# Retention heads of a one-core hybrid block: values and gates requested first, turned outputs stored from SyncE's queue and split half by half, index products one step later, selection steps spread over nearly every step

## The chip, the core and the metric

The kernel runs on one core of one Trainium2 chip. The metric is the device time of one execution in microseconds (us); a smaller number is better. The core's engines each work through their own instructions in order and wait for one another by semaphores: TensorE (PE in the profile, with its weight loads as PEld), VectorE (DVE), ScalarE (ACT), GpSimd (POOL) and SyncE (SP), which only issues DMA transfers here. GpSimd issues transfers too, and computes a little.

## The reference

One block of a language model in float32, for 512 tokens and 16 leading meta tokens, width 1024: a gated feed-forward, a mixer, a second gated feed-forward, and a norm. The mixer adds two branches:

```python
yr = retention(rope(rq), rope(rk) * RET_DK**-0.5, rv)      # 4 heads, keys of 256, values of 512
yr = (jax.nn.silu(rg) * yr) @ w_ret_out                     # yr is normalised per head first
ya = dsa_attention(rope(aq), rope(ak), av, rope(iq), rope(ik), iw, k_top) @ w_att_out
merged = jax.nn.sigmoid(g_ret) * yr + jax.nn.sigmoid(g_att) * ya
h = h + merged @ w_mix_out
```

Retention is attention without a softmax, with a decay in the distance of query and key. The sparse attention first scores all keys by eight small index heads (`relu(iq @ ik) * iw`, summed) and lets each query see its 128 best.

## The kernel before

**Numbers in two parts.** Every float32 operand of a matmul is split into a high part, rounded by ACT (`whi`, line 322), and the rest, by DVE (`wlo`, line 323). A product takes three matmuls: high by high, high by low, low by high. So a weight tile of 128x1024 needs a DMA, an ACT and a DVE instruction before TensorE may use it.

**Steps.** The program from the values' projections to the end of retention is one list of steps (`steps_through`, line 327). A step is one weight tile (128 columns and 8 row blocks, or 256 columns and 4 row blocks): its matmuls, and work of other engines "beside" it. In step i the weights of step i+4 are requested (one request serves two tiles; two buffers called `raw`), those of step i+2 are split, and the lower split is emitted inside the step, by `lower()`. PE, ACT, DVE and, in the part that matters here, SP keep exactly the order in which the code emits (`manual_schedule`); POOL's order is left to the scheduler.

**The stretch of the change** is from about 624 us to 945 us of the profile. Its steps in order: two gate tiles (`psgate`, the gates of the merge); queries and keys of head 1 (`psrq` twice, `psrk` twice); two more gate tiles; then, for each head h, four output steps (`psro`, line 155, called from line 1701) that multiply head h's outputs by `w_ret_out` and add them into eight accumulators `accr`; between the output steps of heads 0, 1, 2 and 3 stand the queries and keys of heads 2 and 3, and before head 3's outputs one tile each of the attention's keys and queries (`psak`, `psaq`) and two gates. While head h is multiplied out, head h+1 is prepared: its gates pass SiLU (`open_gates`), its values are split (`values_in`, line 1487), its keys are roped (`rope_pieces`), its scores decayed (`decayed`, `psst`), and its weighted values computed (`weigh`, `pspv`).

**A head's way out.** `weigh` computes, for four blocks of 128 queries, an output tile in PSUM, its sum of squares (ACT, line 1567) and its product with the gate (DVE, line 1569). After each pair of blocks GpSimd makes the norm's factor (`osum`, line 1574), ACT scales (`normed`), and DVE transposes within 32x32 blocks into `cross` (`turn`, line 1588); four transfers carry `cross` to DRAM (`ots`, lines 1591 and 1592), and one reads it back so that it lies with values on the partitions (`fetch_turned`, `land`, line 1596). `arrived` (line 1752) splits `land` into the two parts of `o`, which the output steps read. A head has two halves of this, `leave_half(h, 0)` from within `weigh_all` and `leave_half(h, 1)` in `trip` (line 1743). The first output matmul reads all 512 tokens of `o`, that is both halves.

**What a head needs first.** `fetch_head` (line 1471) requests a head's values (`vrs`) and gates (`rgs`), 2 MB; `new_decay` its decay table; `place_tails` (line 1367) the meta tokens' values, by GpSimd. For head 0 these stand in `bring_more` and `bring_index`, which the first two gate steps call, with the index heads' queries (`ia`, `ib`: 768 KB each), rope tables and the causal mask.

**Index work.** `index_steps` (line 1298) is a generator: each `pair()` runs one piece, first a small transpose, then ten pieces of four (or eight) matmuls `pssc`, whose results ACT passes through ReLU and DVE adds into `score`. `select_steps` (line 1327) is another: each of its 48 steps, run by `pick(n)`, is a MAX8 and a MATCH_REPLACE8 on DVE that find a row's next eight best scores, sixteen over 512 keys, sixteen over 384, sixteen over 256. What is left of it when the steps end is emitted after them and woven into the attention's start.

PSUM has four banks called `sm` (`pool("mxsm", 4, PSUM)`), which `psgate`, `psrq`, `pssc`, `psst`, `pspv` and `psro` share; a bank is free when ACT or DVE has read it.

## Time and profile before

| | us |
|---|---|
| median of 3 runs | 1543.68 (1543.65 to 1543.93) |
| the profiled execution, its own time | 1542.61 |
| its span, first to last instruction | 1540.8 |
| mean granted clock of TensorE, share of full | 0.984 |
| DVE busy over the span | 1140.2 |
| POOL busy over the span | 213.9 |

The profile of one execution gives for each engine its busy time, for groups of equal instructions their count, total and mean, and for each idle gap what released the engine (written `[idle us <-releaser]`). In the timeline's rows the columns are start, length (both us), engine, line of the kernel, operation, output and input, shape, and the gap before it. Names like `whi<-raw` are the tiles written and read. A row of the view by windows gives the stretch, its length, each engine's busy time with its count, then the granted clock of TensorE (1.00 is full speed), the DMA engines' busy share and GB/s. Lengths of matmul rows overlap, because matmuls are pipelined.

### The profile page before, as it was taken

The page shows a single profiled execution, that of the slowest core. Times are in us where ns is not written, and L with a number is a line of the kernel's source. Part 1 is how long each engine was busy: PE and PEld are TensorE (multiplying, and loading weights), DVE is VectorE, ACT ScalarE, POOL GpSimd, SP SyncE. Part 2 cuts the span into 40 slices and gives each one's busy share as a digit, 9 for nine tenths or more (in the row PEclk, how much of TensorE's full clock was granted, in tenths as well). Part 3 has the DMA queues.
Part 4 walks back from the last instruction along what each step waited for, and adds up shares of the span by engine and source line. Part 5 has one row for each costly group of instructions (what it writes and reads, how often), then busy time and mean ns, then how long its engine had stood idle before and what let it go on. Part 6 is the DMA issues. An engine that isn't in the chain of part 4 may idle for free.

```text
span 1540.8 us, 22309 instructions
## 1 busy us (share of the span) xinstructions
PE 1492.2 (97%) x8704; PEld 1306.3 (85%) x8704; DVE 1140.2 (74%) x1715; ACT 751.3 (49%) x1054; POOL 213.9 (14%) x320
## 2 busy tenths in 40 slices
PE   9999999999999999888989998999999999999997
PEld 8999999999888778776877777988888888888886
DVE  5987585776977877476787868878656787777676
ACT  5555353554454444445433435777634654444343
POOL 1000000002100001220202101344202311111110
PEclk9999999999999999989999999999999999999999
DMA  5233333237554441734335153577568476376423
GB/s 166 74 119 93 100 103 115 85 99 232 184 200 144 154 155 73 256 107 143 86 142 195 52 167 112 141 190 196 170 186 280 133 222 208 109 220 185 140 82 109
DMA packets 169914, 228.42 MB, mean 148 GB/s; under 512 B 18385, under 2 KB 115177, under 8 KB 169553
## 3 DMA queue, kind: packets, MB, share of 16 engines
q1 hardware_dynamic: 147872, 169.77, 34.3%
q0 software_dynamic: 17824, 49.86, 11.3%
q10 hardware_dynamic: 4112, 7.36, 1.4%
q8 instruction: 68, 1.11, 0.3%
q14 instruction: 38, 0.30, 0.1%
HBM read 187.17 MB, written 39.60 MB: 147 GB/s over the span
## 4 chain that ended last, share of the span: by engine, by line
PE 82%; DVE 9%; DMA 4%; ACT 2%; issue 2%; POOL 1%; SPq 0%; POOLq 0%; DVEq 0%; ACTq 0%
PE psqX L2279 7%; PE psd L2444 7%; PE psvX L1196 7%; PE psd L155 7%; PE psqX L155 6%; PE psvY L1196 4%; PE psro L155 4%; PE psqY L2279 4%; PE psqY L155 3%; PE psga L155 3%; PE psat L155 3%; PE psmo L155 3%; PE psak L155 3%; PE psaq L155 2%; DMA raw<-in_w_ret_out_dram 2%
## 5 line engine op out<-in xcount | busy, mean ns | idle before, releaser
L322 ACT ACTIVATE whi<-raw 128x1024 fp32r<-128x1024 f32 (+2 forms) x142 | 133.5, 941 | 137.9 <-PE psd L155 30.9
L323 DVE TENSOR_TENSOR wlo<-raw,whi 128x1024 fp32r<-128x1024 f32 (+2 forms) x142 | 156.1, 1102 | 51.3 <-ACT whi L322 51.3
L323 DVE TENSOR_TENSOR wlo<-w,whi 128x1024 fp32r<-128x1024 f32 x96 | 117.1, 1220 | 64.9 <-ACT whi L322 64.6
L322 ACT ACTIVATE whi<-w 128x1024 fp32r<-128x1024 f32 x96 | 101.6, 1058 | 110.2 <-PE psd L2444 39.3
L155 PE MATMUL psro<-o,whi 128*128 128x512 f32 x256 | 85.4, 414 | 16.7 <-DVE o L323 11.0
L155 PEld LDWEIGHTS psro<-o,whi 128*128 128x128 f32 x256 | 51.5, 201 | 30.3 <-DVE o L323 12.6
L155 PE MATMUL psd<-hl,whi 128*128 128x264 f32 x352 | 71.4, 284 | 0.0
L155 PE MATMUL psd<-hh,wlo 128*128 128x264 f32 x352 | 70.9, 283 | 0.0
L155 PE MATMUL psd<-hh,whi 128*128 128x264 f32 x352 | 70.8, 283 | 0.0
L115 ACT ACTIVATE whi<-raw 128x1024 fp32r<-128x1024 f32 (+1 forms) x42 | 43.5, 1036 | 46.8 <-PE psga L155 11.3
L155 PE MATMUL psqX<-th,whi 128*128 128x264 f32 x216 | 61.2, 283 | 0.2 <-DVE g L543 0.2
L155 PE MATMUL psqX<-tl,whi 128*128 128x264 f32 x216 | 61.2, 283 | 0.0
L155 PE MATMUL psqX<-th,wlo 128*128 128x264 f32 x216 | 61.2, 283 | 0.0
L2444 PE MATMUL psd<-whi,hl 128*128 128x512 f32 (+1 forms) x148 | 56.9, 384 | 0.1
L2444 PE MATMUL psd<-wlo,hh 128*128 128x512 f32 (+1 forms) x148 | 56.8, 384 | 0.0
L2444 PE MATMUL psd<-whi,hh 128*128 128x512 f32 (+1 forms) x148 | 56.8, 384 | 0.0
L116 DVE TENSOR_TENSOR wlo<-raw,whi 128x1024 fp32r<-128x1024 f32 (+1 forms) x42 | 49.9, 1189 | 8.7 <-ACT whi L115 8.6
L287 POOL TENSOR_TENSOR RR<-RR,sq 128x528 f32<-128x528 f32 x7 | 9.4, 1345 | 324.4 <-ACT sq L286 324.4
L155 PEld LDWEIGHTS psd<-hh,wlo 128*128 128x128 f32 x352 | 54.5, 188 | 0.0
L155 PEld LDWEIGHTS psd<-hh,whi 128*128 128x128 f32 x352 | 54.1, 188 | 0.0
L155 PEld LDWEIGHTS psd<-hl,whi 128*128 128x128 f32 x352 | 54.0, 188 | 0.0
L322 ACT ACTIVATE whi<-wsum 128x1024 fp32r<-128x1024 f32 x36 | 38.1, 1060 | 30.2 <-PE psd L155 14.7
(567 smaller groups left out, 4774.0 us busy)
## 6 DMA issues: line engine op xcount, KB each, us to landing
w<-in_w_in_dram SPq DMA_DIRECT2D x40, 512.0 KB, 5.3
raw<-in_w_in_dram SPq DMA_DIRECT2D x27, 512.0 KB, 4.1
raw<-in_w_in_dram SPq DMA_DIRECT2D x13, 1024.0 KB, 6.0
raw<-in_ffn_w_down_dram SPq DMA_DIRECT2D x24, 512.0 KB, 3.9
raw<-in_ffn_w_up_dram SPq DMA_DIRECT2D x11, 1024.0 KB, 5.2
raw<-in_ffn_w_gate_dram SPq DMA_DIRECT2D x10, 1024.0 KB, 5.1
ws<-in_ffn_w_up_dram POOLq DMA_DIRECT2D x20, 512.0 KB, 5.9
w<-in_ffn_w_up_dram SPq DMA_DIRECT2D x20, 512.0 KB, 5.7
```

What stands on the lines that cost most here:

```text
L115: nc.scalar.activation(hi, src, AF.Copy)
L116: eng.tensor_tensor(lo, src, hi.bitcast(F32), ALU.subtract)
L155: nc.tensor.matmul(o, a[:, k, :], b[:, sl], start=first and k == 0 and i == 0, stop=last and k == nk - 1 and i == 2, skip_group_check=onto)
L287: eng.tensor_tensor(ssum[:, :n], ssum[:, :n], sq[:, :n], ALU.add)
L322: nc.scalar.activation(hi, src, AF.Copy)
L323: return lambda: nc.vector.tensor_tensor(lo, src, hi.bitcast(F32), ALU.subtract)
L1196: nc.tensor.matmul(d[bank_][t], a, b[:, k, :], start=not onto and j + k + m == 0, stop=j + k == 3 and m == 2, skip_group_check=onto)
L2279: nc.tensor.matmul(ps[:, t], a, b[:, k, :], start=not onto and j + k + m == 0, stop=j + k == 3 and m == 2, skip_group_check=onto)
L2444: nc.tensor.matmul(ps, a, m[:, j, cs], start=first and i == 0, stop=last and i == 2)
```

## The change

Five edits, all of order or of the issuing queue; no arithmetic changes, and the number of instructions on PE, DVE and ACT stays as it was.

1. Head 0's decay table, values, gates, tails and the index keys are requested in the first gate step; the index queries, the rope tables and the mask in the second.
2. The four stores of a turned half go out on SP's queue instead of GpSimd's, and both read-backs are requested together in `trip`, after the second half's stores.
3. The values, gates and decay table of heads 2 and 3 are requested in the first output step of the head before, as head 1's were, not in `trip`; head 1's decay table moves there too.
4. `arrived` runs half by half: the first half a step earlier, the second where both stood; for head 0 both halves a step earlier (behind the third gate tile).
5. The index pieces start one step later (only the small transpose stays in the last key step) and are spread five to a gate step; selection steps stand in 26 of the 28 steps from head 0's outputs to head 3's, where they stood in 18, and 42 of the 48 come before head 3's outputs, where it was 29.

```diff
         def bring_index():
-            new_decay(0)
             nc.sync.dma_start(ia[:, :, :NL], fq[:, :, :NL])
...
                 nc.sync.dma_start(t, rope[0, i, :, REAL])
+            nc.sync.dma_start(caus, causal)
+            for i, t in enumerate((cos, sin)):
+                nc.sync.dma_start(t, rope[2, i])
 
         def bring_more():
+            new_decay(0)
             fetch_head(0)
+            place_tails(0)
             nc.gpsimd.dma_start(ka[:64, :S], fs[:64, 0, :])
...
             nc.gpsimd.dma_start(iw, fs[64 : 64 + IH, 0, :])
-            place_tails(0)
-            nc.sync.dma_start(caus, causal)
-            for i, t in enumerate((cos, sin)):
-                nc.sync.dma_start(t, rope[2, i])
@@ turn
-                nc.gpsimd.dma_start(d.rearrange("(b i) a e -> a i b e", i=32)[a],
+                nc.sync.dma_start(d.rearrange("(b i) a e -> a i b e", i=32)[a],
@@ outputs, step i
-                        fetch_head(1)
-                    if h == RH - 1 and i == 0:
+                    if i == 0 and h + 1 < RH:
+                        fetch_head(h + 1)
+                        new_decay(h + 1)
+                    elif i == 0:
                         vr["raw"] = fetch_values(4, vraw())
@@
         def leave_half(h, half):
             normed(h, half)
             turn(h, half)
-            fetch_turned(h, half)
@@ beside_outputs
                     some(heads[h + 1]["ropes"]["k"], (4, 3)[i])
-                else:
-                    pick(2)
+                pick((1, h == 0, 1 + (h == 0), 2 + (h == 0))[i])
@@
         def trip(h):
             leave_half(h, 1)
+            for half in range(2):
+                fetch_turned(h, half)
             if h + 1 < RH:
-                if h:
-                    fetch_head(h + 1)
                 place_tails(h + 1)
-                new_decay(h + 1)
 
-        def arrived(h):
-            for low in [turned_parts(h, half) for half in range(2)]:
+        def arrived(h, halves=(0, 1)):
+            for low in [turned_parts(h, half) for half in halves]:
                 low()
@@ the steps
         def start_0(w, lower):
-            bring_index()
+            bring_more()
...
         def start_1(w, lower):
-            bring_more()
+            bring_index()
...
-            arrived(0)
+
+        def after_2(ps):
+            later_gate(2)(ps)
+            arrived(0)
...
-        more += queries_keys(1, (beside_q0, beside_q1, beside_k0, nothing), ((), (), (), ((4, pair), (7, pair))))
-        more += steps_of(gr[2:4], [proj("psgate", REAL, ((1, pair), (3, pair), (5, pair), (7, pair)), later_gate(2)),
-                                   proj("psgate", REAL, ((1, pair), (3, pair), (5, pair), (7, pair)), after_3)])
+        more += queries_keys(1, (beside_q0, beside_q1, beside_k0, nothing), ((), (), (), ((7, pair),)))
+        five = tuple((i, pair) for i in (1, 2, 4, 5, 7))
+        more += steps_of(gr[2:4], [proj("psgate", REAL, five, after_2), proj("psgate", REAL, five, after_3)])
...
-            more += queries_keys(h + 1, (lambda h=h: trip(h), lambda: pick(2), lambda: pick(3), lambda h=h: (arrived(h), pick(1))))
+            more += queries_keys(h + 1, (lambda h=h: (trip(h), pick(2)), lambda: pick(1), lambda h=h: (arrived(h, (0,)), pick(2)),
+                                           lambda h=h: (arrived(h, (1,)), pick(2))))
...
-        more += steps_of(tiles("ak", w_in, OFF_AK, 1), [proj("psak", None, (), lambda ps: (first_kq.append(ps), trip(p)))])
-        more += steps_of(tiles("aq", w_in, OFF_AQ, 1), [proj("psaq", REAL, (), lambda ps: (first_kq.append(ps), pick(2)))])
-        more += steps_of(gr[4:6], [proj("psgate", REAL, (), lambda ps: (later_gate(4)(ps), pick(3))),
-                                   proj("psgate", REAL, (), lambda ps: (later_gate(5)(ps), arrived(p)))])
-        more += outputs(p, lambda i: pick(2 + (i == 0)))
+        more += steps_of(tiles("ak", w_in, OFF_AK, 1), [proj("psak", None, (), lambda ps: (first_kq.append(ps), trip(p), pick(2)))])
+        more += steps_of(tiles("aq", w_in, OFF_AQ, 1), [proj("psaq", REAL, (), lambda ps: (first_kq.append(ps), pick(3)))])
+        more += steps_of(gr[4:6], [proj("psgate", REAL, (), lambda ps: (later_gate(4)(ps), arrived(p, (0,)), pick(4))),
+                                   proj("psgate", REAL, (), lambda ps: (later_gate(5)(ps), arrived(p, (1,)), pick(4)))])
+        more += outputs(p, lambda i: pick(3))
```

How the order on the engines moves is shown at three places. The first is SP's queue in the first two gate steps (`u` is the decay table, `vl` and `g` head 0's values and gates, `ixs` the index queries). Before:

```order
L131 DMA raw<-in_w_in_dram 128x8x256
L1466 DMA u<-in_decay_dram 128x528
L1414 DMA ixs<-fq 128x4x384
L1419 DMA cos<-in_rope_dram 128x512
L1419 DMA sin<-in_rope_dram 128x512
L1479 DMA vl<-vrs 128x1024 x2
L1482 DMA g<-rgs 128x1024 x2
```

and now:

```order
L131 DMA raw<-in_w_in_dram 128x8x256
L1466 DMA u<-in_decay_dram 128x528
L1479 DMA vl<-vrs 128x1024 x2
L1482 DMA g<-rgs 128x1024 x2
L1413 DMA ixs<-fq 128x4x384
L1418 DMA cos<-in_rope_dram 128x512
L1418 DMA sin<-in_rope_dram 128x512
```

The values and gates have moved past the index queries and the index rope tables.

The second place is SP's queue from head 0's last output steps to the first output step of head 1 (`ots<-cross` are the stores, `land<-ots` the read-backs, `in_w_ret_out_dram` the output weights of head 1, `vraw` and `g` the values and gates of head 2). Before:

```order
L1596 DMA land<-ots 128x4x256
L131 DMA raw<-in_w_ret_out_dram 128x4x512
L1596 DMA land<-ots 128x4x256
L1479 DMA vraw<-vrs 128x1024 x2
L1482 DMA g<-rgs 128x1024 x2
L1466 DMA u<-in_decay_dram 128x528
L131 DMA raw<-in_w_ret_out_dram 128x4x512
```

and now:

```order
L1591 DMA ots<-cross 32x16x64 x4
L131 DMA raw<-in_w_ret_out_dram 128x4x512
L1591 DMA ots<-cross 32x16x64 x4
L1596 DMA land<-ots 128x4x256 x2
L131 DMA raw<-in_w_ret_out_dram 128x4x512
L131 DMA raw<-in_w_in_dram 128x8x256
L1479 DMA vraw<-vrs 128x1024 x2
```

The second request of output weights has moved ahead of head 2's values, gates and table, the first ahead of the first read-back; the eight stores are new in this queue.

The third place is ACT's queue around the end of the third gate tile (`RR<-psgate` is the gate's sigmoid, `tmp<-pssc` the ReLU of the index products, `o<-land` the high split of head 0's outputs). Before:

```order
L1319 ACTIVATE tmp<-pssc 128x384 x2
L1656 ACT_TABLE_LOAD
L1656 ACTIVATE RR<-psgate 128x512
L322 ACTIVATE whi<-raw 128x1024
L1319 ACTIVATE tmp<-pssc 128x384 x6
L1319 ACTIVATE tmp<-pssc 128x512 x2
L1656 ACTIVATE RR<-psgate 128x512
```

and now:

```order
L1319 ACTIVATE tmp<-pssc 128x384 x2
L1656 ACT_TABLE_LOAD
L1656 ACTIVATE RR<-psgate 128x512
L322 ACTIVATE o<-land 128x4x256 x2
L322 ACTIVATE whi<-raw 128x1024
L1319 ACTIVATE tmp<-pssc 128x384 x6
L1319 ACTIVATE tmp<-pssc 128x512 x4
```

The two splits of head 0's outputs now stand ahead of the last ten ReLUs, where they stood behind the last.

## The prediction

> **What bounds the kernel now.** I read the page's busy shares first, then TensorE's idle gaps in the stretch that the change touches, then the granted clock behind them, then who was late.
>
> ```profile
> PE 1492.2 (97%) x8704; PEld 1306.3 (85%) x8704; DVE 1140.2 (74%) x1715; ACT 751.3 (49%) x1054; POOL 213.9 (14%) x320
> ```
>
> TensorE is busy 97% of the span, so nothing can be won outside its gaps, unless matmuls run slowly. The timeline of PE from 640 to 950 us shows nearly all gaps of the program's middle:
>
> ```profile
> 650.74 0.80 PE L1563 MATMUL pspv<-vh,ph 128*128 128x512 f32 x1 [4.02 <-ACT vh L1491]
> 684.17 0.80 PE L1315 MATMUL pssc<-ikh,iq 128*128 128x512 f32 x1 [5.15 <-DVE iq L1449]
> 685.96 0.79 PE L1315 MATMUL pssc<-ikh,iq 128*128 128x512 f32 x1 [0.56 <-DVE iq L1449]
> 711.66 0.56 PE L155 MATMUL psro<-o,whi 128*128 128x512 f32 x1 [2.97 <-ACT o L322]
> 715.08 0.79 PE L155 MATMUL psro<-o,whi 128*128 128x512 f32 x1 [2.85 <-DVE o L323]
> 779.06 0.80 PE L155 MATMUL psro<-o,whi 128*128 128x512 f32 x1 [4.74 <-DVE o L323]
> 843.11 0.50 PE L155 MATMUL psro<-o,whi 128*128 128x512 f32 x1 [2.84 <-DVE o L323]
> 864.33 4.37 PE L1538 MATMUL psst<-rqk 128*128 128x256 f32 x18 [2.38 <-DVE accr L1710]
> 907.07 0.79 PE L155 MATMUL psro<-o,whi 128*128 128x512 f32 x1 [2.72 <-ACT o L322]
> 945.28 0.63 PE L1924 MATMUL psS<-ak,aq 128*128 128x400 f32 x2 [1.82 <-ACT aq L115]
> 947.79 3.28 PE L1924 MATMUL psS<-ak,aq 128*128 128x400 f32 x13 [1.88 <-DVE aq L116]
> ```
>
> The first nine add up to 28.2 us, the last two to 3.7. Each gap is also followed by a slow run. The view by windows, cut to those runs, has length, busy PE and, third from the end, the granted clock:
>
> ```profile
> 650.74:657.28 6.54, 6.08 (x13) 4.47 (x14) 5.81 (x7) 2.94 (x4) 0.00 (x0) 0.50 0.27 96
> 684.17:691.28 7.11, 6.55 (x17) 4.96 (x18) 4.37 (x4) 3.68 (x6) 0.00 (x0) 0.50 0.01 1
> 715.08:718.65 3.57, 3.57 (x8) 2.81 (x9) 3.54 (x5) 0.48 (x1) 0.00 (x0) 0.50 1.04 357
> 779.06:783.49 4.43, 4.43 (x10) 3.47 (x11) 3.87 (x7) 1.06 (x1) 0.00 (x0) 0.50 0.68 225
> 843.11:848.00 4.89, 4.89 (x22) 4.05 (x22) 1.76 (x4) 1.06 (x1) 0.00 (x0) 1.00 0.59 198
> 864.33:869.17 4.84, 4.84 (x20) 3.19 (x21) 4.06 (x9) 1.77 (x4) 0.00 (x0) 0.65 0.33 115
> 908.44:913.30 4.86, 4.86 (x11) 3.80 (x12) 4.53 (x10) 0.00 (x0) 0.00 (x0) 0.50 0.29 118
> ```
>
> Busy PE times the missing share of the clock is lost: 3.0, 3.3, 1.8, 2.2, 0, 1.7 and 2.4 us, 14.4 in all. So gaps and what follows them hold 46 us, 3% of the kernel; everything that can be won is there. I go through them in the program's order.
>
> **1. Head 0's values (part 1 of the change).** SP's first request of the stretch, ACT's rows before the first gap, and a DVE row behind it:
>
> ```profile
> 624.54 0.37 SPq L131 DMA_DIRECT2D raw<-in_w_in_dram  x1
> 643.64 1.28 ACT L1498 ACT_TABLE_LOAD   x1
> 647.03 1.06 ACT L1498 ACTIVATE g<-g 128x1024 f32<-128x1024 f32 x1 [2.11 <-DMA g<-rgs]
> 648.68 1.06 ACT L1498 ACTIVATE g<-g 128x1024 f32<-128x1024 f32 x1 [0.60 <-DMA g<-rgs]
> 658.26 1.34 DVE L1569 TENSOR_TENSOR g<-pspv,g 128x512 f32<-128x512 f32 x2
> ```
>
> The gates land too late by 2.11 + 0.60 = 2.7 us, and the split of the values stands behind them. The weight request went out at 624.5, the second gate landed at 648.7: 24 us for the 4.5 MB from the one to the other in SP's queue (weights 1.0, decay 0.26, index queries 0.75, two tables 0.5, values and gates 2.0). Now 3.3 MB are, which at that rate land after 17.7 us, at 642.2, ahead of the end of the table load at 644.9. So the 2.7 us go. The index tables, now behind, land by 648.7 by the same sum, and DVE comes to them behind the values' lower split, which begins at 648 and takes over 2 us. What is late next is DVE: the product of the fourth block needs the bank that `g` of the first frees, at 658.26 + 0.7 - 2.7 = 656.3, and PE, which starts at 648.0, is there some 6 us later (21 matmuls of 0.23 at full clock, and the wait for the first lower split). So PE gains what DVE gains: **-2.8** (0 if the gates land as late as before, -5.7 if DVE were not in the way).
>
> **2. Index products (parts 2 and 5).** POOL, DVE, and PE's first matmul behind the weighted values:
>
> ```profile
> 662.96 2.63 POOL L1591 DMA_DIRECT2D ots<-cross  x4 [2.41 <-DVE cross L1588]
> 665.60 0.73 POOL L1574 TENSOR_TENSOR osum<-osum,mhalf 128x2 f32<-128x2 f32 x1
> 663.68 0.16 DVE L1573 TENSOR_SCALAR osum<-osum 128x2 f32<-128x2 f32 x1
> 662.10 0.40 PE L155 MATMUL psrq<-xh,whi 128*128 128x512 f32 x1
> 682.37 3.54 DVE L1449 TENSOR_TENSOR iq<-ixs,iq 64x1536 fp32r<-64x1536 f32 x2 [1.55 <-ACT iq L1446]
> ```
>
> The norm's factor was ready to be made at 663.84, but POOL first issued four stores, to 665.59. With the stores on SP it starts 1.75 us sooner, and the chain from there to `iq` is DVE and ACT back to back. The first half of `iq` (682.37 + 1.75) came 22.0 us after 662.1, now 20.25. PE had 16.9 us of other work in that time (684.17 - 5.15 - 662.1); the pair now stands behind two more groups of three matmuls, 1.4 us. So the gap shrinks from 5.71 to about 2.5: **-3.2**, and, if the clock stays up behind so short a gap, **-3.3** more (both 0 if the chain isn't shortened, -9 if no gap is left).
>
> **3. Head 0's outputs (part 4).** PE's first matmul of the fourth gate tile, and ACT's rows of the third place of the orders:
>
> ```profile
> 698.70 0.39 PE L155 MATMUL psgate<-xh,whi 128*128 128x512 f32 x1
> 700.03 0.60 ACT L1656 ACTIVATE RR<-psgate 128x512 f32<-128x512 f32 x1
> 701.47 1.69 ACT L1319 ACTIVATE tmp<-pssc 128x384 f32<-128x384 f32 x4
> 709.46 2.15 ACT L322 ACTIVATE o<-land 128x1024 fp32r<-128x1024 f32 x2
> ```
>
> The gaps of 2.97 + 2.85 = 5.82 and the 1.8 of slow clock go, since `o` is split about 10 us before its use. But a new wait takes part of their place. Counted from the fourth tile's start (698.7): its second index pair needs a bank that the first pair's ReLU frees, which began at +2.8 and ended at +3.3. Now two splits (2.03 from start to start) stand ahead of it, so it ends at +5.3, and PE, with the pair moved from k=3 to k=2, is there at +2.4: 2.9 us. Net **-4.7** (0 to -7.6). In head 0's output steps DVE has three selection steps more, 1.5 us each (the row below, with the replace of equal length); I take its slack there as 3 us, and put **+1.0** (0 to +4.5).
>
> **4. Heads 1 and 2 (parts 2, 3, 4).**
>
> ```profile
> 766.26 1.06 ACT L322 ACTIVATE whi<-raw 128x1024 fp32r<-128x1024 f32 x1 [1.51 <-DMA raw<-in_w_ret_out_dram]
> 846.18 1.06 ACT L322 ACTIVATE whi<-raw 128x1024 fp32r<-128x1024 f32 x1 [8.20 <-DMA raw<-in_w_ret_out_dram]
> 776.65 2.35 DVE L323 TENSOR_TENSOR o<-land,o 128x1024 fp32r<-128x1024 f32 x2
> L1334 DVE MAX8 top<-score 128x8 f32<-128x512 f32 x6 | 4.2, 692 | 0.1
> ```
>
> The first matmul of an output step needs both halves, so splitting by halves alone frees nothing: before the split's end stand five selection steps, as before. What goes is DVE's idle time on the way: 1.3 us by POOL's earlier factor (as in 2, now filled by a selection step) and 1.5 on the late weights, whose request now precedes the read-back. Following DVE's order, I get the split of head 1 done at 776.5 instead of 779.0: gap 4.74 to 2.2, and the clock's 2.2 with it; but DVE gains only some 3 us by the decayed scores, so about 1.7 come back there. Head 1: **-3.0**. For head 2: gap 2.84 to 1.45; the 8.20 us that ACT waited for weights queued behind 2 MB of values go, and with them 1.5 of the 2.38 and the 1.7 of slow clock: **-4.6**. Both lie between 0 and their whole gaps, -7 each.
>
> **5. Head 3 and the attention's start (parts 4, 5).** ACT's last split for head 3 is now one half, 1.05 us shorter, and the clock may stay up: **-3.4** (0 to -5.7). Behind it, DVE's group from 929 to 952 us:
>
> ```profile
> L1335 DVE MATCH_REPLACE8 score<-top,score 128x256 f32<-128x256 f32 x12 | 4.9, 408 | 0.0
> ```
>
> Twelve replaces and as many MAX8 of about that length, some 9.5 us, are woven there between DVE's instructions, ahead of the late `aq`; they now come earlier, where DVE waits. **-2.5** of the 3.7 (0 to -5).
>
> **Sum.** -2.8 - 6.5 - 4.7 + 1.0 - 3.0 - 4.6 - 3.4 - 2.5 = -26.5. Against it: I leave five gaps of 2.2 to 2.9 us. Of the five gaps of 2.3 to 3.0 us in the rows, three were followed by slow clock, which cost 1.8, 1.7 and 2.4; five times 0.6 times 2.0 is **+6**. So -20.5. From the profiled execution's 1542.6 that is 1522.1; the median of the runs lies 1.1 above it, so **1523**.
>
> The Trainium skill's page "TensorE: Matmul & The Clock Gate", in its Part 1 on the clock gate, says that a free-running window of about 3.4 us decides, and that an idle window halves the clock. By that rule alone none of my remaining gaps would cost clock, and the sum would be that of rival A. The trace has a row against it, 2.38 us idle and 0.65 behind, and one for it, 2.84 idle and 1.00 behind.
>
> **What SP's new work costs.** The eight stores a head cost SP's queue an issue each (0.66 us on POOL by the row 662.96); all that waits behind them is weights used 11 us later and the read-backs. I cost them at nothing; if that cover is gone, ACT waits for weights as at 846.18.
>
> **Rivals.** A, the clock stays up behind the shorter gaps: -26.5, 1517. The rows behind 843.11 speak for it, those behind 864.33 against.
>
> B, DVE paces: gaps reappear wherever DVE is late, and only what shortens its own chain counts: 2.7 (values), 1.75 (factor), 2.5, 1.4, and 2.5 at the attention: -10, about 1533. For it speaks that nearly all gaps name DVE, and its work is unchanged; against it, that its idle time in these stretches is waiting for ACT, DMA and POOL.
>
> C, slower: the values of a head come too late. They are requested about 10.5 us before ACT splits them, while the next weights load.
>
> ```profile
> vraw<-vrs SPq DMA_DIRECT2D x2, 512.0 KB, 7.9
> 728.52 2.00 ACT L1491 ACTIVATE vh<-vraw 128x1024 fp32r<-128x1024 f32 x2
> ```
>
> Head 1's, requested so already (at 711.3), landed in 7.9, well before their use at 728.5. In the full queues at 630 such transfers took 18. At 18 each of three heads would be 7.5 late, ACT with it and then PE, and 2.2 of clock behind each: +29, so 1552. It decides from about 15 us of landing on.
>
> D, the change doesn't do what it says: the halves, the earlier splits and the earlier picks move waits about and the sum stays within 3 us: 1542.
>
> **How the numbers follow.** Forecast 45%, A 20%, B 18%, D 7%, C 10%. The range reaches from 1508 (A with the larger ends of terms 2 and 4) to 1538 (B with half its terms gone); outside lie C, D and a little of A's far side. About 0.2%, 3 us, is what a measurement of this kernel can tell from no change. Faster: 0.83; same: 0.07; slower: 0.10.
>
> **What would show it.** In the changed profile: no DMA releaser ahead of the gates' SiLU in head 0, and PE's first gap about 1.3 us; a wait of `pssc` on ACT of about 2.9 us in the fourth gate step; psro's gaps at 0, 2.2, 1.5 and 2.3 us for heads 0 to 3; no long ACT wait for `in_w_ret_out`; no selection among the attention's first DVE rows. A wait of `vh` on DMA for heads 1 to 3 would make it wrong, or granted clock of 0.50 behind most of the remaining gaps.

## The result, and the profile after

| | before | after |
|---|---|---|
| median, us (four runs each, on one chip) | 1543.66 | 1518.97 (1518.00 to 1520.19) |
| the profiled execution, its own time and span, us | 1542.61, 1540.8 | 1518.44, 1516.5 |
| mean granted clock | 0.984 | 0.992 |

The ratio is 0.9842, with a 95% interval from 0.9825 to 0.9859: 24.7 us less. The page's first line and the timeline of PE over the same stretch, after:

```profile
PE 1483.9 (98%) x8704; PEld 1300.1 (86%) x8704; DVE 1143.6 (75%) x1715; ACT 750.5 (49%) x1054; POOL 192.7 (13%) x288
```

```profile
647.30 0.51 PE L1563 MATMUL pspv<-vh,ph 128*128 128x512 f32 x1 [1.22 <-ACT vh L1491]
648.56 0.50 PE L1563 MATMUL pspv<-vl,ph 128*128 128x512 f32 x1 [0.75 <-DVE vl L1493]
655.66 0.50 PE L1563 MATMUL pspv<-vh,ph 128*128 128x512 f32 x1 [0.64 <-DVE g L1569]
679.20 0.50 PE L1315 MATMUL pssc<-ikh,iq 128*128 128x512 f32 x1 [2.12 <-DVE iq L1449]
680.99 0.80 PE L1315 MATMUL pssc<-ikh,iq 128*128 128x512 f32 x1 [1.06 <-DVE iq L1449]
696.62 0.45 PE L1315 MATMUL pssc<-ikh,iq 128*128 128x384 f32 x1 [2.82 <-ACT tmp L1319]
725.74 3.00 PE L1538 MATMUL psst<-rqk 128*128 128x256 f32 x18 [1.38 <-ACT accr L1710]
766.71 0.50 PE L155 MATMUL psro<-o,whi 128*128 128x512 f32 x1 [1.96 <-DVE o L323]
786.93 2.97 PE L1538 MATMUL psst<-rqk 128*128 128x256 f32 x18 [1.39 <-DVE accr L1712]
828.09 0.50 PE L155 MATMUL psro<-o,whi 128*128 128x512 f32 x1 [1.43 <-DVE o L323]
847.24 2.97 PE L1538 MATMUL psst<-rqk 128*128 128x256 f32 x18 [0.32 <-DVE accr L1712]
887.78 0.50 PE L155 MATMUL psro<-o,whi 128*128 128x512 f32 x1 [1.70 <-ACT o L322]
889.67 0.79 PE L155 MATMUL psro<-o,whi 128*128 128x512 f32 x1 [1.39 <-DVE o L323]
```

Three things are to be seen. The gap of 4.0 us ahead of head 0's values is down to 1.2, and the two ahead of head 0's outputs (2.97 and 2.85) are gone; a new wait on ACT's ReLU stands at 696.62, and one of 1.38 at head 1's scores (725.74); ahead of head 3's outputs 3.09 us are left, where 2.72 and 0.58 stood. The attention's two gaps of 1.8 and 1.9 us do not appear any more.

How much earlier the same matmul of PE starts says where the time went. At the beginning of the stretch the two traces are already 0.64 us apart.

| first matmul of | before | after | earlier by | won since the row above |
|---|---|---|---|---|
| head 1's second query tile | 662.10 | 658.75 | 3.35 | 2.7 |
| head 2's queries (behind head 0's outputs) | 751.50 | 741.93 | 9.57 | 6.2 |
| head 3's queries (behind head 1's outputs) | 817.46 | 803.85 | 13.61 | 4.0 |
| the attention's keys (behind head 2's outputs) | 882.06 | 863.78 | 18.28 | 4.7 |
| the gate behind head 3's outputs | 932.42 | 914.14 | 18.28 | 0.0 |
| the second gate in the attention's start | 960.08 | 935.91 | 24.17 | 5.9 |

### The profile page after: what moved, and what is told of

It reads as the page before. It is cut to its first block, busy times and chain, and to the rows that moved or that the text cites. A ratio compares the mean times of both kernels' runs of the same rounds, so it can differ in the third digit from the quotient of the medians.

```text
span 1516.5 us, 22282 instructions
## 1 busy us (share of the span) xinstructions
PE 1483.9 (98%) x8704; PEld 1300.1 (86%) x8704; DVE 1143.6 (75%) x1715; ACT 750.5 (49%) x1054; POOL 192.7 (13%) x288
## 4 chain that ended last, share of the span: by engine, by line
PE 86%; DVE 9%; ACT 3%; issue 2%; DMA 0%; POOL 0%; POOLq 0%; DVEq 0%; ACTq 0%
PE psd L155 8%; PE psd L2447 8%; PE psqX L2282 7%; PE psqX L155 7%; PE psvX L1196 7%; PE psvY L1196 4%; PE psqY L2282 4%; PE psqY L155 3%; PE psga L155 3%; PE psat L155 3%; PE psmo L155 3%; PE psak L155 3%; PE psaq L155 3%; PE psgate L155 2%; PE psrq L155 2%; PE psro L155 2%
## 5 line engine op out<-in xcount | busy, mean ns | idle before, releaser
L155 PE MATMUL psro<-o,whi 128*128 128x512 f32 x256 | 81.9, 400 | 6.5 <-DVE o L323 4.8
L155 PE MATMUL psro<-o,wlo 128*128 128x512 f32 x128 | 50.9, 398 | 0.0
```

The lines of the kernel that those rows point to most:

```text
L155: nc.tensor.matmul(o, a[:, k, :], b[:, sl], start=first and k == 0 and i == 0, stop=last and k == nk - 1 and i == 2, skip_group_check=onto)
```

## The experiments

The kernel before ran beside each set, so versions of different sets are compared by their ratios to it. The changed kernel stands at 0.9842 and, run again later, at 0.9856.

| version | median, us | ratio to before, 95% interval |
|---|---|---|
| changed, values behind the index queries again (edit 1 undone) | 1519.28 | 0.9854 (0.9836 to 0.9872) |
| changed, stores on GpSimd again (edit 2 undone) | 1520.41 | 0.9866 (0.9848 to 0.9884) |
| changed, heads 2 and 3 fetched later again (edit 3 undone) | 1518.70 | 0.9852 (0.9833 to 0.9871) |
| changed, halves split together again (edit 4 undone) | 1522.26 | 0.9876 (0.9860 to 0.9892) |
| changed, selection as before (that part of edit 5 undone) | 1531.10 | 0.9930 (0.9908 to 0.9952) |
| changed, unaltered, second time | 1520.11 | 0.9856 (0.9837 to 0.9874) |
| new: head 3's splits | 1513.67 | 0.9818 (0.9803 to 0.9832) |
| new: and head 0's splits | 1512.50 | 0.9810 (0.9796 to 0.9825) |
| new: and no selection between splits | 1507.99 | 0.9778 (0.9763 to 0.9793) |
| that one, edit 1 undone | 1509.63 | 0.9791 (0.9775 to 0.9806) |
| that one, ten selection steps left over | 1513.23 | 0.9813 (0.9796 to 0.9831) |
| that one, index pieces later | 1505.84 | 0.9763 (0.9748 to 0.9779) |

### Edit 1 undone

```diff
-            bring_more()
+            bring_index()
             proj("psgate", REAL, (), later_gate(0))(w, lower)
@@ and the reverse in the second gate step, with the two functions as before
```

> The changed kernel with edit 1 undone: the index queries and tables are again requested in the first gate step, head 0's table, values, gates and tails in the second. Theory (the values' landing set the first gap): a gap of about 4 us with a transfer as its releaser is back ahead of head 0's weighted values and the clock drops behind it, while the index part stays as it is in the changed kernel: 3 to 5 us more than the changed kernel, about 1522.5. Rival (the next wait, DVE's index queries, takes up whatever is lost before it): within 1 us of 1519.

ACT's rows of the changed kernel, and then of this one:

```profile
644.30 2.01 ACT L1498 ACTIVATE g<-g 128x1024 f32<-128x1024 f32 x2
646.21 1.99 ACT L1491 ACTIVATE vh<-vl 128x1024 fp32r<-128x1024 f32 x2
```

```profile
647.60 1.06 ACT L1498 ACTIVATE g<-g 128x1024 f32<-128x1024 f32 x1 [2.23 <-DMA g<-rgs]
649.41 1.06 ACT L1498 ACTIVATE g<-g 128x1024 f32<-128x1024 f32 x1 [0.76 <-DMA g<-rgs]
...
651.47 0.50 PE L1563 MATMUL pspv<-vh,ph 128*128 128x512 f32 x1 [4.30 <-ACT vh L1491]
```

The two waits for the gates are back, 2.99 us, and PE's gap is 3.08 longer. Yet the time is that of the changed kernel, which is neither the 3 to 5 us of the theory nor what the rival gives as its reason: the index products waited 2.13 us as before, and PE was still 3.18 us later at head 3's outputs (889.26 for 886.08), of which 1.08 already lay between the two traces at 640 us, ahead of the edit. At head 3, and behind the wait at `pssc`, this execution simply had no slow clock. The time alone settles nothing here, so I tried the edit again in the version of 1508 us, which has fewer gaps:

> The fastest version so far, the one without selection between the splits (1508 us), with edit 1 undone. Undoing edit 1 in the changed kernel made the first gap 3.1 us longer in the trace and left the time as it was, since other gaps cost less slow clock there. Theory (the 3.1 us are on the path, and the slow clock behind the other gaps came out differently by chance, with the place of the gaps on a fixed grid of the clock): here, with fewer gaps left that can slow the clock, 3 to 4.5 us more, 1511 to 1512.5. Rival (a wait later in the program takes the 3.1 us up): 1508 again, and the events behind the last output step come no later.

The gap was 3.97 us for 1.22, the next 0.46 for 0.76, 2.45 together. The time rose by 1.6 us (2.0 by the ratios), less than the theory's lower end of 3; the intervals overlap. The rival's 1508 lies as near as the theory's 1511, but no later wait took the delay up, as the rival has it: the attention's first transposes start 2.6 us later than without the edit (925.23 for 922.60). What the trace shows is some 2.5 us, at the edge of what a measurement of times can tell; the slow clock behind this gap added nothing, for a reason that comes below.

### Edit 2 undone

```diff
-                nc.sync.dma_start(d.rearrange("(b i) a e -> a i b e", i=32)[a],
+                nc.gpsimd.dma_start(d.rearrange("(b i) a e -> a i b e", i=32)[a],
```

> The changed kernel with only the stores of a turned half back on GpSimd's queue. Theory: head 0's second half's sums on GpSimd stand behind four stores again and hold DVE's chain, so the index products start 1.7 us later, and about 1.3 us go at heads 1 and 2: 2 to 4 us more than the changed kernel, about 1522. Rival (DVE has room, or SP's queue was the better place without the eight stores per head): within 1 us of 1519, or below it.

POOL and PE:

```profile
660.64 2.63 POOL L1591 DMA_DIRECT2D ots<-cross  x4 [2.41 <-DVE cross L1588]
663.28 0.73 POOL L1574 TENSOR_TENSOR osum<-osum,mhalf 128x2 f32<-128x2 f32 x1
...
681.86 0.50 PE L1315 MATMUL pssc<-ikh,iq 128*128 128x512 f32 x1 [3.77 <-DVE iq L1449]
773.42 0.50 PE L155 MATMUL psro<-o,whi 128*128 128x512 f32 x1 [3.46 <-DVE o L323]
```

The factor stands behind four stores again, and the gap at the index products is 3.77 for 2.12 us: 1.65 more, as the theory had it. Ahead of head 1's outputs it is 3.46 for 1.96; ahead of head 2's it stayed 1.43, so the 1.3 us there were not lost. The median rose by 1.4 us (1.5 to 3.7 by the two ratios), at the theory's lower end.

### Edit 3 undone

```diff
-                    if i == 0 and h + 1 < RH:
-                        fetch_head(h + 1)
-                        new_decay(h + 1)
+                    if i == 0 and h == 0:
+                        fetch_head(1)
@@ trip
+                if h:
+                    fetch_head(h + 1)
                 place_tails(h + 1)
+                new_decay(h + 1)
```

> The changed kernel with edit 3 undone: values, gates and decay tables of heads 2 and 3 are requested again in the step behind the head's outputs. Theory: the output weights of heads 1 and 2, queued behind 2 MB, land late again and DVE and ACT fall behind: gaps ahead of head 1's and head 2's outputs near 3 us where they are 1.96 and 1.43: 3 to 6 us more than the changed kernel, with slow clock in part of it. Rival (the stores moved to SP's queue already put those weights ahead of the 2 MB, or they have time enough): gaps as in the changed kernel, within 1 us.

ACT, and PE's gaps at head 1's outputs and behind head 2's:

```profile
766.74 1.06 ACT L322 ACTIVATE whi<-raw 128x1024 fp32r<-128x1024 f32 x1 [4.87 <-DMA raw<-in_w_ret_out_dram]
...
766.39 0.50 PE L155 MATMUL psro<-o,whi 128*128 128x512 f32 x1 [1.96 <-DVE o L323]
847.79 2.96 PE L1538 MATMUL psst<-rqk 128*128 128x256 f32 x18 [1.18 <-DVE accr L1711]
```

The theory fell. The weights do land late again, and ACT waits 4.87 us for them; but the split that waits is for a later output step, with nothing urgent behind it on ACT, and head 1's gap is 1.96 as before. Only the scores behind head 2's outputs wait longer, 1.18 for 0.32. The time is the same. A long wait of ACT with a transfer as its releaser was no evidence that PE paid for it.

### Edit 4 undone

```diff
         def after_3(ps):
             later_gate(3)(ps)
+            arrived(0)
@@ after_2
-            arrived(0)
@@ heads 1 and 2, and alike for head 3
-            lambda h=h: (arrived(h, (0,)), pick(2)), lambda h=h: (arrived(h, (1,)), pick(2))
+            lambda: pick(2), lambda h=h: (arrived(h), pick(2))
```

> The changed kernel with both halves of a head's outputs split again in one step, at the place where they stood before the change (for head 0 behind the fourth gate tile). Theory: ahead of head 0's outputs the gap of about 5.8 us and its 1.8 us of slow clock return, and the wait of the index products behind the splits (2.8 us and 1.7 us of slow clock) goes, so 3 us; heads 1 to 3 lose about 1 us each where the first half's split no longer stands ahead: 4 to 6 us more, about 1524. Rival (the early splits bought nothing, since what they took from head 0's outputs they gave to the index products): within 1 us of 1519.

PE ahead of head 0's outputs:

```profile
707.52 0.51 PE L155 MATMUL psro<-o,whi 128*128 128x512 f32 x1 [2.77 <-ACT o L322]
710.06 0.80 PE L155 MATMUL psro<-o,whi 128*128 128x512 f32 x1 [2.04 <-DVE o L323]
```

The gaps come to 4.81 us (5.8 expected), with a stretch at half clock to 715.7 behind them; the wait at `pssc` fell from 2.82 to 0.70, and the wait of 1.38 at head 1's scores went. Heads 1 and 2 lost nothing: 1.52 and 0.99 us for 1.96 and 1.43. Net 3.3 us by the medians, 3 to 5 by the ratios. The edit pays, all of it at head 0.

### Selection

```diff
@@ beside_outputs
-                pick((1, h == 0, 1 + (h == 0), 2 + (h == 0))[i])
+                if i >= 2:
+                    pick(2)
@@ queries and keys of heads 2 and 3: 0, 2, 3, 1 for 2, 1, 2, 2; ak, aq and gates 0, 2, 3, 0 for 2, 3, 4, 4
-        more += outputs(p, lambda i: pick(3))
+        more += outputs(p, lambda i: pick(2 + (i == 0)))
```

> The changed kernel with the selection steps where they stood before the change (29 ahead of head 3's outputs, where the changed kernel has 42). Theory: the 5.9 us that the attention's start became shorter are lost again, and heads 1 and 2, whose gaps end on DVE, get back 1 to 3 us: 3 to 5 us more, about 1523. Rival (DVE sets the pace of the heads, so selection steps cost there what they save later): within 1 us of 1519, the gaps ahead of head 1's and head 2's outputs and scores under 1 us.

This one part cost 12 us by the medians, half of what the whole change won. Its four runs spread widely, from 1527.1 to 1532.9, and in the profiled one, 14 us longer than the changed kernel's, 2.3 us were lost to half clock ahead of head 0's outputs, before any selection step had run; so 10 to 12 us belong to the selection. First PE, then DVE behind head 1's last transpose and in the attention's start, then DVE in the changed kernel's start of the attention:

```profile
770.85 0.50 PE L155 MATMUL psro<-o,whi 128*128 128x512 f32 x1 [3.56 <-DVE o L323]
...
934.39 0.63 PE L1928 MATMUL psS<-ak,aq 128*128 128x400 f32 x2 [1.82 <-ACT aq L115]
936.90 3.34 PE L1928 MATMUL psS<-ak,aq 128*128 128x400 f32 x13 [1.88 <-DVE aq L116]
```

```profile
750.98 1.23 DVE L323 TENSOR_TENSOR wlo<-raw,whi 128x1024 fp32r<-128x1024 f32 x1 [1.78 <-ACT whi L322]
...
932.00 0.67 DVE L1294 TENSOR_TENSOR tmp<-tmp,sin 128x512 f32<-128x512 f32 x1
932.59 0.08 DVE L1335 MATCH_VALUE_LOAD score<-top,score 128x8 f32 x1
932.66 0.41 DVE L1335 MATCH_REPLACE8 score<-top,score 128x256 f32<-128x256 f32 x1
932.99 0.68 DVE L1295 TENSOR_TENSOR tmp<-tmp 128x512 f32<-128x512 f32 x1
```

```profile
923.02 0.68 DVE L1294 TENSOR_TENSOR tmp<-tmp,sin 128x512 f32<-128x512 f32 x1
923.73 0.69 DVE L1295 TENSOR_TENSOR tmp<-tmp 128x512 f32<-128x512 f32 x1
```

In the attention's start a piece of selection stands between almost any two instructions that lead to `aq`, and the scores wait for `aq`. The theory's second half was the wrong way round: heads 1 and 2 got nothing back on balance. Their gaps grew to 3.56 and 3.10 us, and the waits at the scores behind them shrank only from 1.39 and 0.32 to 0.30 and nothing. Ahead of head 1's second split there are five selection steps in both kernels. But in the changed one two of the five run where DVE here sits idle for 1.78 us (the row at 750.98), and here three, not two, stand directly between the two splits. So places count, not numbers. (In the changed kernel the 48 steps are used up after the second of head 3's four output steps, so the last two calls there find nothing to do.) The attention's part alone, on the version of 1508 us:

> The version of 1508 us without selection steps in head 3's output steps, so that ten are left over to the attention's start. Theory (the 5.9 us that the attention's start gained came from the selection that no longer stands there): two gaps of about 1.8 us ahead of the attention's scores with a clock drop behind them, 4 to 6 us more, about 1513, and nothing changed before. Rival (its gain came from something else, and the leftover steps pass beside other work): within 1 us of 1508.

The same two gaps of 1.82 and 1.88 us came back, with granted clock 0.53 and 0.50 in the two stretches of 3.4 us from 916.3 on. It cost 5.2 us, within the theory's 4 to 6; the rival is out.

### The clock

> The changed kernel unaltered, on the same chip as the three versions beside it, to stand them against. Theory and rival alike: the time that it had, 1519 us, or as much less as the kernel before reads less on this chip; the same gaps as in its first trace. If slow-clock stretches lie behind other gaps than in the first trace, the clock's answer to a gap is not fixed by the order of the instructions.

The gaps were those of the first trace to within 0.04 us, and the stretches at half clock lay behind the same gaps. Their ends gave the clue: in the first trace matmuls go back to full speed at 653.5, 684.1, 701.2 and 895.8, which lie 9, 5 and 57 times 3.41 us apart. So the view by windows, cut every 3.41 us from a point near one such end (in this trace the cuts lie some 0.3 us ahead of the changes of the granted clock, hence 0.55 and 0.54 for 0.50); three groups of windows of the changed kernel (busy PE is the second number, granted clock the third from the end):

```profile
646.20:649.61 3.41, 1.55 (x6) 1.06 (x7) 2.33 (x3) 2.94 (x4) 0.65 (x1) 1.00 1.04 364
649.61:653.03 3.42, 3.42 (x10) 2.70 (x9) 3.14 (x5) 0.21 (x1) 0.18 (x1) 0.55 0.58 206
...
762.25:765.67 3.42, 2.50 (x20) 2.16 (x19) 3.35 (x6) 1.06 (x1) 0.00 (x0) 1.00 0.00 0
765.67:769.08 3.41, 2.37 (x10) 1.99 (x11) 3.31 (x7) 0.00 (x0) 0.00 (x0) 1.00 0.74 222
769.08:772.49 3.41, 3.41 (x16) 2.82 (x15) 3.38 (x5) 0.00 (x0) 0.00 (x0) 1.00 1.02 357
...
885.13:888.55 3.42, 1.45 (x6) 0.63 (x4) 3.28 (x9) 2.44 (x3) 0.55 (x1) 1.00 0.13 50
888.55:891.96 3.41, 2.29 (x5) 1.82 (x6) 3.24 (x9) 0.12 (x1) 0.00 (x0) 0.54 0.80 255
891.96:895.38 3.42, 3.42 (x9) 2.64 (x8) 3.32 (x9) 0.00 (x0) 0.00 (x0) 0.50 0.55 232
```

The version with head 3's splits at the gap of 1.96 us, and the one with edit 1 undone at head 3:

```profile
764.43:767.85 3.42, 1.46 (x7) 1.22 (x7) 3.35 (x6) 0.70 (x1) 0.00 (x0) 1.00 0.42 99
767.85:771.26 3.41, 3.41 (x9) 2.62 (x9) 3.38 (x6) 0.00 (x0) 0.00 (x0) 0.51 1.08 390
```

```profile
887.67:891.08 3.41, 1.71 (x9) 1.09 (x7) 3.24 (x10) 1.78 (x3) 0.55 (x1) 1.00 0.00 0
891.08:894.49 3.41, 2.02 (x8) 1.43 (x9) 3.31 (x8) 0.78 (x1) 0.00 (x0) 1.00 0.72 225
894.49:897.90 3.41, 3.41 (x17) 2.81 (x16) 3.27 (x9) 0.00 (x0) 0.00 (x0) 1.00 0.76 314
```

One and the same gap of 1.96 us is cut in two by the grid in the changed kernel, and the clock stays up; in the next version it lies within one window, which leaves 1.46 us of work, and the following window runs at half speed. It is alike with the gaps of 1.70 and 1.39 at head 3: with 1.97 us of them in one window they cost clock, parted into 1.70 and 1.39 they did not. I laid such a grid over the stretch from 640 to 945 us of all fourteen traces, each cut where its own granted clock changes. Of the windows that began at full speed, 42 were followed by one at half speed and 1,132 were not. All 39 in which PE idled 1.8 us or more were among the 42; the other three had 1.55 to 1.72 us, and the largest idle time that cost nothing was 1.79. With all cuts 0.3 us earlier, as in the rows of the changed kernel above, the two kinds overlap from 1.6 to 2.1 us. So the edge lies a little over half a window, and these traces do not fix it to better than some 0.3 us. The grid's place differed from execution to execution. What no experiment did was to shift it on purpose.

The Trainium skill's page "TensorE: Matmul & The Clock Gate" gives in its Part 1 a free-running window of about 3.4 us; the traces agree with that length (changes of the clock at multiples of 3.41 us), but not with the need of a whole idle window, since PE worked during a part of 41 of the 42 windows, and somewhat more than half a window was enough.

### Better versions

Head 3's halves ahead of what held them:

```diff
-        proj("psgate", REAL, (), lambda ps: (later_gate(4)(ps), arrived(p, (0,)), pick(4))),
-        proj("psgate", REAL, (), lambda ps: (later_gate(5)(ps), arrived(p, (1,)), pick(4)))
+        proj("psgate", REAL, (), lambda ps: (pick(4), later_gate(4)(ps), arrived(p, (0,)))),
+        proj("psgate", REAL, ((3, lambda: arrived(p, (1,))),), lambda ps: (later_gate(5)(ps), pick(4)))
```

> The changed kernel with head 3's second half split within the sixth gate step (ahead of that gate's sigmoid), and the four selection steps of the fifth gate step put ahead of the first half's split. Theory (the two gaps of 1.70 and 1.39 us ahead of head 3's outputs are ACT's queue behind the sigmoid and DVE's behind four selection steps): both gaps go, and with them the 3.0 us of slow clock: 3 to 6 us less than the changed kernel. Rival (the read-back lands too late for an earlier split, or the score steps that follow take up the gain): the gaps move to another wait of about 3 us, same time.

The second half's split on ACT and DVE in the changed kernel, and then ACT, DVE and PE here:

```profile
886.61 1.12 ACT L322 ACTIVATE o<-land 128x1024 fp32r<-128x1024 f32 x1
888.40 1.22 DVE L323 TENSOR_TENSOR o<-land,o 128x1024 fp32r<-128x1024 f32 x1
```

```profile
882.88 1.12 ACT L322 ACTIVATE o<-land 128x1024 fp32r<-128x1024 f32 x1
...
884.03 1.23 DVE L323 TENSOR_TENSOR o<-land,o 128x1024 fp32r<-128x1024 f32 x1 [0.74 <-ACT o L322]
...
656.82 0.50 PE L1563 MATMUL pspv<-vh,ph 128*128 128x512 f32 x1 [2.27 <-DVE g L1569]
894.81 0.73 PE L155 MATMUL psro<-o,whi 128*128 128x512 f32 x2 [0.83 <-DVE accr L1712]
```

Both gaps went, 0.83 us on the accumulators came, and the time fell by 6.4 us against the changed kernel beside it: a little above the theory's upper end. The row at 656.82 also says why the stretch at half clock from 649.9 to 653.3 in the changed kernel cost nothing. Here that run is missing, and PE waits 2.27 us for DVE where it waited 0.64: the slow clock had eaten time that PE would have idled.

Then head 0's halves within the fourth gate step, at its row blocks 3 and 6, between the index pieces:

```diff
         def after_2(ps):
             later_gate(2)(ps)
-            arrived(0)
...
-                                   proj("psgate", REAL, five, after_3)])
+                                   proj("psgate", REAL, halved, after_3)])   # five, and each half at 3 and 6
```

> As the one with head 3's splits, and head 0's two halves split within the fourth gate step between its index pieces, where the changed kernel has both ahead of them. Theory: the 2.8 us wait of the index products on ACT goes with its 1.7 us of slow clock, no wait comes ahead of head 0's outputs, and the wait of 1.4 us at head 1's scores is as it was: 2.8 to 4.5 us less than with head 3's splits alone. Rival (DVE paces the fourth gate step, so the wait returns ahead of head 0's outputs): within 1 us.

PE at the index products and at head 0's outputs:

```profile
696.15 0.44 PE L1315 MATMUL pssc<-ikh,iq 128*128 128x384 f32 x1 [0.70 <-ACT tmp L1319]
704.53 0.50 PE L155 MATMUL psro<-o,whi 128*128 128x512 f32 x1 [0.73 <-DVE o L323]
```

The wait of 2.74 became 0.70, but 0.73 came at the outputs, and this wait had cost no clock in the trace it is compared with. It won 1.2 us, between theory and rival. Then the two selection steps between the splits of heads 1 and 2 went to head 3's output steps:

```diff
-            lambda h=h: (arrived(h, (0,)), pick(2))
+            lambda h=h: arrived(h, (0,))
```

> As the one with head 0's and head 3's splits, and without the two selection steps that stand between the two halves' splits of heads 1 and 2; these four go to head 3's output steps. Theory (DVE paces the way into the outputs): the gaps of 1.96 and 1.43 us ahead of head 1's and head 2's outputs go: 3.4 us less. Rival (the next wait, of the scores on the accumulators, grows by what goes here): the gaps of 1.39 and 0.32 us at the scores grow to 2 to 3 us and the time stays within 1 us.

The gaps of 1.96 and 1.43 us are gone, and those at the scores did not grow (0.71 for 1.36, none for 0.32). It won 4.5 us, more than the theory's 3.4, and the rival is out. Last, the index pieces of the third gate step at row blocks 3 to 7:

```diff
-        proj("psgate", REAL, five, after_2)
+        proj("psgate", REAL, tuple((i, pair) for i in (3, 4, 5, 6, 7)), after_2)
```

> The version of 1508 us with the five index pieces of the third gate step at its row blocks 3 to 7, where they stand at 1, 2, 4, 5 and 7. Theory (the first piece asks for its split queries 2.1 us before DVE has them): the gaps of 2.13 and 1.05 us shrink to about 0.8 and 0.3 and the slow clock of 1.5 us behind them goes; 2 to 3.5 us less, about 1505. Rival (the pieces, packed together, wait on ACT's ReLU and the four banks, or the fourth gate step ends later on DVE): the gaps reappear there and the time stays within 1 us.

PE at the first piece:

```profile
681.12 0.50 PE L1315 MATMUL pssc<-ikh,iq 128*128 128x512 f32 x1 [0.55 <-DVE iq L1449]
```

The first gap is 0.55 for 2.13, the second stayed at 1.05, and no window behind them is slow: 2.2 us less, within the theory's 2 to 3.5, though the two intervals overlap. At 1505.84 us, ratio 0.9763 (0.9748 to 0.9779), this is the fastest, 14.3 us below the changed kernel's second run.

## Why the prediction was right, and where it was not

It gave 1523 in a range from 1508 to 1538; the time is 1518.97, between the forecast and rival A. Rivals C and D are out: no head's values were waited for, and the sum moved by 24 us. Rival B was half right: what is left names DVE, and the better versions won by moving DVE's work.

1. **Values, -2.8: right.** 2.7 in the trace, and the reason too: no gate is waited for, and a DVE chain is late next. That it put no clock on this gap was right for a reason it did not have: a stretch at half clock is free where a later wait would have taken the time.
2. **Index products, -6.5, and head 0's outputs, -4.7 and +1.0: mechanisms right, less won.** Forecast was 10.2 ahead of the allowance; 6.2 came. The gap shrank by 2.5 (5.71 to 3.18, 3.2 forecast), and about 1.5 of the slow clock behind it stayed. The new wait on ACT measured 2.82 for the 2.9 worked out, and cost 1.7 of clock, which only the allowance covered. The wait at head 1's scores is 1.38, for the +1.0 put down for head 0's output steps. The stores' part, 1.75, measured 1.65.
3. **Heads 1 and 2, -3.0 and -4.6: sizes right, one step wrong.** They won 4.0 and 4.7, and the gaps came out at 1.96 and 1.43 for 2.2 and 1.45. But "1.5 on the late weights" failed at head 1: with the weights late again the gap was unchanged. In its place stands the selection: with its old places the gap was 1.60 longer. At head 2 the late weights were worth 0.86 of the 1.5 us. That no slow clock followed head 1's gap of 1.96 was the grid's place, so luck, but little hung on it: in the version with head 3's splits it did follow, and the wait of 1.39 at the scores behind it went in turn.
4. **Head 3, -3.4: wrong.** Nothing was won. The step that failed is "ACT's last split for head 3 is now one half, 1.05 us shorter": so it is, but DVE's split behind it had four selection steps put ahead of it, and ACT's stayed behind the gate's sigmoid; with both moved, both gaps went. The gaps were 3.09 us for the 2.3 forecast, and two slow windows followed.
5. **Attention's start, -2.5: the mechanism right, mis-sized.** 5.9 us came, and leaving ten steps there cost 5.2 again: both gaps whole, and the slow clock behind them, which the term had not counted.
6. **The allowance of +6 for the clock was nearly the right size**, 7.9 us in stretches at half clock after (1.7 behind the values, which cost nothing, 1.5 at the index products, 1.7 at the wait on ACT and 3.0 at head 3, each busy PE times the missing clock). How it was made up was less sound. Its own terms leave four gaps of 2.2 to 2.9 us (2.5, 2.9, 2.2 and 2.3), not five, and of the five gaps in its rows four were followed by slow clock, not three: behind the one at 711.66 the half clock had begun at 711.9 (granted 0.51 from 711.84 to 715.25). Nor is it a coin for each gap, but a rule with a place. With the edge taken as 1.8 us, a lone gap of 2.5 us is caught in a share of (3.41 + 2.5 - 2 x 1.8) / 3.41 = 0.7 of the grid's places and costs at most 1.7 us, by estimate 1.2 on the mean; the allowance had 0.6 x 2.0.
7. **SP's new work, costed at nothing: right.** The eight stores of head 1 took 4.7 us of SP's queue (1.95 and 2.74), and ACT waited for no transfer in the whole stretch.

The part that was undervalued is the selection, which the prediction weighed with +1.0 and -2.5 and which alone carries 10 to 12 of the 24 us. Of the other four edits the undoing says less. The first is worth some 2 us in the version of 1508 us, while the changed kernel was level without it; the second 1.5 to 3.7; the third 0 to 1.5; the fourth 3 to 5. What is left, a few us, these runs cannot assign: the index pieces' new places, the other part of the fifth edit, were not undone alone.

## What to carry to other kernels

Small background work on an engine is worth placing by what the engine waits for at each point: of five steps ahead of a split, two cost nothing while they stood inside a wait of DVE. With those two behind the wait, and one step more between the two splits that a matmul needed, its gap was 1.6 us longer. A wait in the profile counts only if TensorE, or whoever sets the end, is late because of it; here ACT waited 4.9 us for a transfer at no cost. And a gap is cheaper than it looks or dearer by 1.7 us of slow clock, depending on whether about 1.8 us of idle time fall into one window of 3.41 us, so gaps are best broken up or brought below that.

## What the runs showed of the hardware that was not expected

The granted clock changed only on a grid of 3.41 us, which stayed fixed through an execution and lay elsewhere in the next. Idle time of about 1.8 us in one window, not a whole window's, was enough to halve the clock in the following one: 2.1 us or more always did, 1.5 us or less never did, and between the two the outcome depends on where the cuts are taken to lie. A window at half speed was followed by another where PE idled more than 0.85 us in it, and by a full one where it idled less than 0.4; between these both occurred. This also bounds what a comparison of two single traces can say: the version with edit 1 undone had a gap 3.1 us longer and came out level, because the grid cut the wait at `pssc` in two and parted the two gaps at head 3.
